# Adding up the modulation's partial sums: small TensorE products, or a round trip through device memory and VectorE

## The chip, the cores and the metric

The kernel runs on one core of one Trainium2 chip. The metric is device time in microseconds (us), the median of several runs. TensorE is called PE in the views of the profile, VectorE DVE, ScalarE ACT, GpSimd POOL, SyncE SP.

## The reference

A decoder trunk of two layers over a sequence of 256 rows of width 1024. Each layer has three sub-layers: a SwiGLU of width 2816, a token mixer (half spatial gating, half attention over selected keys), and a second SwiGLU. Each is normalised and modulated by a vector made from the condition `c`:

```
c_act = silu(c)
mod = c_act @ ada_w[l] + ada_b[l]                    # 1024 -> 9 * 1024
sh1, sc1, g1, sh2, sc2, g2, sh3, sc3, g3 = split(mod, 9)
h = rms_norm(x, norm) * (1 + sc) + sh
x = x + gate * sublayer(h)                           # gate is 0.5*g1, g2, 0.5*g3
```

The change concerns only `c_act @ ada_w`, a product of one row with a matrix of 1024 x 9216 per layer.

## The kernel before, in words

**The stream of weights.** All weights come in an order that is fixed in a list (`seq`). SP loads them in tiles of 128 x 1024 into seven buffers (`raw`). A tile of a matrix product is split in two parts: ScalarE rounds it to the coarser format (`whi`, line 535), and VectorE computes the rest (`wlo`, line 540). Both go into a ring of ten slots (`NB`), a slot being free again when the second half of the sequence has used it. PE multiplies with three products for each pair of tiles (high by high, high by low, low by high).

**The two halves.** The 256 rows are two halves of 128, 0 and 1. In the up projections of a SwiGLU (`joint_chunk`) both are multiplied together, 256 columns wide; in the down projection and the mixer they go apart, half 0 up to seven items ahead of half 1 (`LAG`), after which the halves alternate. One step of such a generator is an item: one weight tile for one half (in the joint part for both). In the down projection an item is six matmuls.

**The modulation.** Vector by vector (A is the scale, B the shift, G the gate, with the number of the sub-layer), eight tiles of `ada_w` stand between the weight tiles in the list. Partition p holds the rows 8p to 8p+7 of the matrix, so each engine operation multiplies a tile by a column of `c_act` and adds it to an accumulator `aacc` of 128 x 1024 (ScalarE's line 517 for the first, VectorE's line 522 for the others). What is left is to add `aacc` over the 128 partitions. Layer 0's A1 and B1 are made in `start` in another way; the other sixteen vectors, ten of kind A or B and six of kind G, are finished as follows.

- `fold_rows` (line 409): two items after the last tile, VectorE's transposing reduce (line 414) turns `aacc` into `R`, 128 x 32: within each block of 32 partitions the sums over those 32, so that four partial sums stand on four groups of partitions.
- Ten items later PE multiplies `R` by a constant 0/1 matrix `fold`, which adds the four groups: `col_finish` (line 458) for A and B, whose result has to stand with the width over the partitions, and `ada_finish` (line 423) for G. The result lies in a PSUM bank.
- One item after that VectorE takes it out. For A and B it picks each partition's own quarter (lines 466, 469) and adds bias and norm weight (`col_bias`). For G it adds a row of biases, loaded earlier by POOL (line 420), POOL writes the row to device memory (`gline`, line 435) and loads it back spread to all partitions (`vec`, line 437), and the residual update uses it (line 645).

Work like this is put off with `defer(n, ...)`: it is written into the program n items later. The program order is therefore fixed by these counts; each engine carries out its own instructions in that order.

**What stands around it.** In the first SwiGLU of layer 0 POOL also makes the tables of the rotary embedding, one step after each item (`rope_tables`, lines 179 to 227): POOL and VectorE take turns (the tile `nf` is written by POOL, line 194, and cast by VectorE, lines 196 and 198). There too the weights of the spatial gating are loaded and masked by POOL (`sgu_prep`, line 877) and transposed by PE some items later (line 885, four matmuls of line 117 on `xm`). POOL also computes the reciprocal roots of the norms (line 618). PSUM has eight banks, handed out in turn by `take` and `give`; the gates of the SwiGLU empty them (lines 797 and 798).

**Line 575 and PE's streams.** `mm3r` writes 512 columns in a strided order; after any other matmul, or after 48 of its own (`PERIOD`), it puts in one group in plain order, with the second product cut in two of 256 columns.

Of the kernel before, what the change touches and what calls it, by code (L numbers as in the profile page):

```python
# [9 lines left out]
F32 = mybir.dt.float32  # L10
# [3 lines left out]
ALU = mybir.AluOpType  # L14
AX = mybir.AxisListType

P = 128
D = 1024
KD = D // P
# [10 lines left out]
SPREAD = (1, 2, 1)  # L30
TAIL = 3
VX = 188
FOLD_D = (2, 2, 10)
ADA_DL = 8
D_EVP = 0
D_V = 0
# [4 lines left out]
EV_D = 1  # L41
# [60 lines left out]
def trunk(ctx, tc, x_in, c_in, pos_in, ada_w, ada_b, norm_ffn1, ffn1_w_in, ffn1_w_out,  # L102
# [3 lines left out]
    V, S, G = nc.vector, nc.scalar, nc.gpsimd  # L106
# [11 lines left out]
    T = Counted()  # L118
    ctx.enter_context(tc.manual_schedule())
    const = ctx.enter_context(tc.tile_pool(name="const", bufs=1))  # L120
    small = ctx.enter_context(tc.tile_pool(name="small", bufs=2))
# [3 lines left out]
    vecp = ctx.enter_context(tc.tile_pool(name="vecp", bufs=NV))  # L125
    dramp = ctx.enter_context(tc.tile_pool(name="dramp", bufs=2, space=bass.MemoryType.DRAM))
# [10 lines left out]
    def give(*ts):  # L137
        banks.extend(ts)
# [5 lines left out]
    ident = const.tile([P, P], F32, name="ident")  # L144
# [4 lines left out]
    S.activation(ccol, c_raw, AF.Silu)  # L149
    negm = const.tile([P, 2 * P], F32, name="negm")  # L150
    V.memset(negm, 1.0)
    fold = const.tile([P, P], F32, name="fold")
    mconst = const.tile([P, 16], F32, name="mhalf")
    mhalf, quarter = mconst[:, :1], mconst[:, 4:8]
    G.memset(mhalf, -0.5)

    def fold_setup():
        V.tensor_reduce(quarter, ident.rearrange("p (a c) -> p a c", a=4), axis=AX.X, op=ALU.add)
        V.tensor_reduce(fold[:, :32], ident.rearrange("p (a c) -> p c a", a=4), axis=AX.X, op=ALU.add)
        V.tensor_copy(fold[:, 32:].rearrange("p (a c) -> p a c", a=3),  # L160
                      fold[:, None, :32].to_broadcast([P, 3, 32]))

    def causal_mask():
        G.memset(negm, 0.0)
# [66 lines left out]
    cols = const.tile([P, DEPTH, 96], F32, name="cols")  # L231
    ab = const.tile([P, DEPTH, 3, 2, KD], F32, name="ab")
    accs = [None]
# [14 lines left out]
    def spare_tile(i):  # L248
        n_sp[i] += 1
        q = n_sp[i] % 3  # L250
        return spare[i][:, 32 * q:32 * q + 32]
# [100 lines left out]
    vec = {}  # L352
    pend = []

    def defer(n, fn):
        pend.append([n, fn])
# [49 lines left out]
                    :, j, v * D:(v + 1) * D])  # L406
            dp[0] += 1

    def fold_rows(acc, then):
        R = spare_tile(0)  # L410
        blocks = acc.rearrange("p (j r) -> p j r", r=32)

        def red():
            V.tensor_reduce(R, blocks, axis=AX.X, op=ALU.add, apply_transpose=True)
            then(R)
        defer(FOLD_D[0], red)

    def bias_row(e):
        row = spare_tile(1)[:32]
        G.dma_start(row, ada_b[e["l"], e["v"] * D:(e["v"] + 1) * D].rearrange("(j r) -> j r", r=32))  # L420
        accs.append(row)

    def ada_finish(e, acc):
        l, v = e["l"], e["v"]
        row = accs.pop()

        def go(R):
            def prod():
                ps = tp_tile()
                T.matmul(ps[:32, :32], R, fold[:, :32], start=True, stop=True)  # L430

                def put():
                    V.tensor_tensor(row, ps[:32, :32], row, op=ALU.add)
                    line = dramp.tile([1, D], F32, name="gline", tag="gline")
                    G.dma_start(line.rearrange("o (j r) -> (o j) r", r=32), row)
                    t = vecp.tile([P, D], F32, name="vec", tag="vec")
                    G.dma_start(t, line.to_broadcast([P, D]))
                    vec[(l, "G", v // 3 + 1)] = t
                evac_later(EV_D, put)
            defer(FOLD_D[2], prod)  # L440
        fold_rows(acc, go)

    have = set()

    def col_bias(l, i, kind, cs, k0):
        n = cs.shape[-1]
        v = (i - 1) * 3 + (kind == "A")
        bias = cols[:, l, v * KD + k0:v * KD + k0 + n]
        have.add((l, i, kind))
        if kind == "A":  # L450
            gn = cols[:, l, 72 + (i - 1) * KD + k0:72 + (i - 1) * KD + k0 + n]
            dst = ab[:, l, i - 1, 0, k0:k0 + n]
            V.scalar_tensor_tensor(dst, cs, 1.0, bias, op0=ALU.add, op1=ALU.add)
            V.tensor_tensor(dst, dst, gn, op=ALU.mult)
        else:
            V.tensor_tensor(ab[:, l, i - 1, 1, k0:k0 + n], cs, bias, op=ALU.add)

    def col_finish(e, acc, late):
        def go(R):
            def prod():  # L460
                ps = tp_tile()
                T.matmul(ps[:, :32], fold, R, start=True, stop=True)

                def put():
                    Rk = R.rearrange("p (k m) -> p k m", m=4)
                    V.tensor_tensor(Rk, ps[:, :32].rearrange("p (k m) -> p k m", m=4),
                                    quarter[:, None, :].to_broadcast([P, KD, 4]), op=ALU.mult)
                    cs = small.tile([P, KD], F32, name="cs", tag="cs")
                    V.tensor_reduce(cs, Rk, axis=AX.X, op=ALU.add)
                    col_bias(e["l"], e["v"] // 3 + 1, e["kind"], cs, 0)  # L470
                evac_later(EV_D, put)
            defer(FOLD_D[2] + late, prod)
        fold_rows(acc, go)

    late = []

# [11 lines left out]
    def pump(quota=2, force=False, now=False, hi_only=False):  # L488
        dma_fill()
        if hold[0] > 0 and not (force or now):  # L490
            return
        if not hi_only:
            pump_lo()
        while sp[0] < len(seq) and quota > 0:
            e = seq[sp[0]]
            if hi_only and e["k"] != "w":
                break
            if e["k"] == "s":
                if "done" not in e:
                    break  # L500
                sp[0] += 1
                continue
            need = e["k"] == "w"
            r = len(ring)
            if e["k"] == "w" and not force and len(W) - wcur[0] >= lead[0]:
                break
            if need and r >= NB and not ring[r - NB]:
                assert not force, (r, ring[r - NB:], wcur, [q[0] for q in pend])
                break
            if e["k"] == "a":  # L510
                j = e["j"]
                if j == 0:
                    aacc = accs[0] = aap.tile([P, D], F32, name="aacc", tag="aacc")
                    if e["kind"] == "G":
                        bias_row(e)
                    if ADA0_ACT:
                        S.activation(aacc, e["raw"], AF.Copy, scale=ccol[:, 0:1])
                    else:
                        V.tensor_scalar(aacc, e["raw"], ccol[:, 0:1], None, op0=ALU.mult)
                else:  # L520
                    aacc = accs[0]
                    V.scalar_tensor_tensor(aacc, e["raw"], ccol[:, j:j + 1], aacc,  # L522
                                           op0=ALU.mult, op1=ALU.add)
                if j == KD - 1 and e["kind"] == "G":
                    ada_finish(e, aacc)
                elif j == KD - 1:
                    col_finish(e, aacc, ADA_DL if (e["kind"], e["v"]) == ("A", 7) else 0)
            if need:
                ring.append(False)
                hi = hlp.tile([P, D], F32R, name="whi", tag="whi")  # L530
                lo = hlp.tile([P, D], F32R, name="wlo", tag="wlo")
                n = e["kt"] * e["cols"]
                src = e["raw"][:, :n]
                quota -= 1
                S.activation(hi[:, :n], src, AF.Copy)  # L535
                if hi_only:
                    late.append((e, hi, lo, r))
                    sp[0] += 1
                    continue
                V.tensor_tensor(lo[:, :n], src, hi[:, :n].bitcast(F32), op=ALU.subtract)  # L540
                e["hi"], e["lo"], e["slot"] = hi, lo, r
                W.append(e)
            sp[0] += 1
            n_rd[0] += 1
            dma_fill()
# [302 lines left out]
    def tp_tile():  # L848
        m = tp_n[0]
        tp_n[0] += 1  # L850
        if m - 2 in tp_ev:
            tp_ev.pop(m - 2)()
        t = tp_bank[m] = take()
        return t

    def evac_later(n, fn, tiles=1):
        done = []
        mine = range(tp_n[0] - tiles, tp_n[0])

        def run():  # L860
            if not done:
                done.append(1)
                fn()
                give(*[tp_bank.pop(m) for m in mine])
        for m in mine:
            tp_ev[m] = run
        if n is not None:
            defer(n, run)
        return run
# [393 lines left out]
    def start(env):  # L1263
# [73 lines left out]
        next(gb)  # L1337
        hold[0] = 0
        causal_mask()
        fold_setup()  # L1340

    gens = {}
    for pi, (kind, l, i, n) in enumerate(phases):
# [89 lines left out]
```

## Time and profile before

| | us |
|---|---|
| median of 3 runs | 979.49 |
| lowest, highest | 978.81, 979.78 |
| the profiled execution | 978.13 |
| its span in the trace | 976.40 |
| PE busy | 961.0 (98%) |
| VectorE busy | 768.7 (79%) |
| ScalarE busy | 530.1 (54%) |
| GpSimd busy | 54.8 (6%) |

The granted clock of TensorE was 0.999 of full speed. All moments are microseconds from the span's start. A row of the timeline gives start, duration, engine, line, operation, what it writes and reads, and, where the engine stood idle before, how long and what ended it. Matmuls overlap, so that two rows' starts, not their durations, tell how fast PE goes. A row of the stretches gives for each engine the busy time and the count of instructions, then the granted clock, the busy share of the DMA engines and the rate in GB/s. A row of the DMA issues gives the count, the size and the median time from issue to landing.

### The profile page before, as it was taken

Reading aid. Unit: us, or ns where it says so; the run is one execution under the profiler, and the core shown is the slowest. Engines: PE = TensorE matmul, PEld = TensorE weight load, DVE = VectorE, ACT = ScalarE, POOL = GpSimd, SP = SyncE. Lnnn points to the kernel's source line nnn. Section 1 sums busy time; section 2 is a strip of 40 time slices with the busy share of each in tenths; the row PEclk is TensorE's granted clock in tenths of the full one; section 3 lists DMA queues with packets and bytes.
Section 4 is the critical chain, followed back from the end, with each engine's and each line's share of the span. In section 5 each row is a group of like instructions: output and inputs, shape, how many; then the busy total and the mean of one; then the engine's idle time right before and its main releaser. Section 6 shows DMA issues by size and latency. Waiting matters only on the chain.

```text
span 976.4 us, 16690 instructions
## 1 busy us (share of the span) xinstructions
PE 961.0 (98%) x6448; PEld 866.6 (89%) x6448; DVE 768.7 (79%) x1072; ACT 530.1 (54%) x794; POOL 54.8 (6%) x92
## 2 busy tenths in 40 slices
PE   7999999999999999999999999999999999999997
PEld 6899998887888899998889999988777889999886
DVE  6889899788998888786587898767899886656444
ACT  6565555375676754553366554345657775444331
POOL 4012400000000100000000100000000000000000
PEclk9999999999999999999999999999999999999999
DMA  9989999967665799897868999885765557777431
GB/s 330 393 277 364 337 385 377 413 178 230 185 181 172 229 329 348 314 328 252 262 185 299 329 332 318 302 301 173 246 189 184 170 175 250 247 239 235 151 129 43
DMA packets 110416, 253.47 MB, mean 260 GB/s; under 512 B 9138, under 2 KB 27620, under 8 KB 110336
## 3 DMA queue, kind: packets, MB, share of 16 engines
q1 hardware_dynamic: 108256, 248.06, 74.6%
q0 software_dynamic: 1792, 3.82, 1.2%
q8 instruction: 50, 0.82, 0.3%
q10 hardware_dynamic: 288, 0.52, 0.1%
q14 instruction: 30, 0.25, 0.1%
HBM read 251.30 MB, written 1.07 MB: 258 GB/s over the span
## 4 chain that ended last, share of the span: by engine, by line
PE 85%; DVE 6%; DMA 4%; issue 2%; ACT 1%; POOL 0%; SPq 0%; POOLq 0%; DVEq 0%; ACTq 0%
PE bank L113 83%; PE bank L117 2%; DMA raw<-in_ffn_w_in_dram 2%; DVE wlo L540 2%; DMA sraw<-in_ada_w_dram 1%; DVE aacc L1195 1%; DVE aacc L522 1%; ACT whi L535 1%; DMA raw<-in_ada_w_dram 1%; DVE xm L645 0%; DVE xm L635 0%; DVE x L647 0%; DVE wlo L481 0%; POOL rstd L618 0%; DVE hTlo L641 0%
## 5 line engine op out<-in xcount | busy, mean ns | idle before, releaser
L535 ACT ACTIVATE whi<-raw 128x1024 fp32r<-128x1024 f32 (+1 forms) x328 | 340.2, 1050 | 261.9 <-PE bank L113 167.1
L540 DVE TENSOR_TENSOR wlo<-raw,whi 128x1024 fp32r<-128x1024 f32 (+1 forms) x313 | 375.1, 1211 | 112.1 <-ACT whi L535 110.6
L113 PE MATMUL bank<-hThi,whi 128*128 128x256 f32 x1216 | 325.0, 278 | 1.4 <-ACT hThi L1233 0.9
L113 PE MATMUL bank<-hThi,wlo 128*128 128x256 f32 x1216 | 322.0, 276 | 0.0
L113 PE MATMUL bank<-hTlo,whi 128*128 128x256 f32 x1216 | 322.0, 276 | 0.0
L113 PEld LDWEIGHTS bank<-hThi,whi 128*128 128x128 f32 x1216 | 222.4, 188 | 3.5 <-ACT hThi L1233 1.5
L113 PEld LDWEIGHTS bank<-hTlo,whi 128*128 128x128 f32 x1216 | 222.1, 188 | 0.1
L113 PEld LDWEIGHTS bank<-hThi,wlo 128*128 128x128 f32 x1216 | 222.0, 188 | 0.0
L522 DVE SCALAR_TENSOR_TENSOR aacc<-raw,ccol,aacc 128x1024 f32<-128x1024 f32 x112 | 143.5, 1281 | 0.0
L113 PE MATMUL bank<-whi,aThi 128*128 128x512 f32 (+1 forms) x374 | 141.0, 377 | 0.0
L113 PE MATMUL bank<-whi,hThi 128*128 128x512 f32 (+1 forms) x352 | 140.4, 399 | 0.0
L113 PE MATMUL bank<-wlo,aThi 128*128 128x512 f32 (+1 forms) x404 | 140.1, 359 | 0.0
L113 PE MATMUL bank<-whi,aTlo 128*128 128x512 f32 (+1 forms) x374 | 139.8, 374 | 0.0
L113 PE MATMUL bank<-whi,hTlo 128*128 128x512 f32 (+1 forms) x352 | 135.4, 385 | 0.2
L113 PE MATMUL bank<-wlo,hThi 128*128 128x512 f32 (+2 forms) x374 | 134.3, 369 | 0.0
L113 PEld LDWEIGHTS bank<-wlo,aThi 128*128 128x128 f32 x404 | 75.9, 188 | 13.0
L113 PEld LDWEIGHTS bank<-wlo,hThi 128*128 128x128 f32 x374 | 70.5, 188 | 12.1
L113 PEld LDWEIGHTS bank<-whi,aTlo 128*128 128x128 f32 x374 | 70.3, 188 | 11.1
L113 PEld LDWEIGHTS bank<-whi,aThi 128*128 128x128 f32 x374 | 70.2, 188 | 10.9
L113 PEld LDWEIGHTS bank<-whi,hTlo 128*128 128x128 f32 x352 | 66.1, 188 | 14.0 <-DVE hTlo L641 1.1
L113 PEld LDWEIGHTS bank<-whi,hThi 128*128 128x128 f32 x352 | 66.3, 188 | 13.6 <-issue 2.0
L798 DVE TENSOR_TENSOR xm<-xm,bank 128x256 f32<-128x256 f32 x76 | 29.6, 417 | 38.8 <-ACT xm L797 38.8
(166 smaller groups left out, 680.9 us busy)
## 6 DMA issues: line engine op xcount, KB each, us to landing
raw<-in_ffn_w_in_dram SPq DMA_DIRECT2D x160, 512.0 KB, 5.4
raw<-in_ada_w_dram SPq DMA_DIRECT2D x128, 512.0 KB, 5.5
raw<-in_ffn_w_out_dram SPq DMA_DIRECT2D x88, 512.0 KB, 5.8
raw<-in_mix_w_in_dram SPq DMA_DIRECT2D x40, 512.0 KB, 4.4
sraw<-in_ada_w_dram SPq DMA_DIRECT2D x32, 256.0 KB, 5.8
raw<-in_ffn_w_in_dram SPq DMA_DIRECT2D x32, 256.0 KB, 4.2
raw<-in_mix_w_out_dram SPq DMA_DIRECT2D x16, 512.0 KB, 4.1
vec<-gline POOLq DMA_DIRECT2D x6, 512.0 KB, 7.2
```

The source lines that it names most:

```text
L113: return nc.tensor.matmul(*a, **kw)
L117: return nc.tensor.transpose(*a, **kw)
L522: V.scalar_tensor_tensor(aacc, e["raw"], ccol[:, j:j + 1], aacc, op0=ALU.mult, op1=ALU.add)
L535: S.activation(hi[:, :n], src, AF.Copy)
L540: V.tensor_tensor(lo[:, :n], src, hi[:, :n].bitcast(F32), op=ALU.subtract)
L798: V.tensor_tensor(a, a, acc[j][:, 256:], op=ALU.mult)
L1195: V.scalar_tensor_tensor(acc, su[g][j], ccol[:, j:j + 1], su["dps"] if j == PEJ else acc, op0=ALU.mult, op1=ALU.add)
```

## The change

The products with `fold` go, and with them the constants `fold` and `quarter`, their setup, the bank that each took, and the loading of the bias rows. In their place `column_sums`, for all sixteen vectors: behind the transposing reduce POOL writes `R` to a table `part` in device memory, 128 x 32, and with four loads, one for each quarter of the columns, brings to every partition the four partial sums of its own eight columns (`C`, 128 x 32, pieces of 32 bytes). Eleven items after the reduce (`FOLD_D[1]`; nineteen for A3, which was put off by eight items before as well) VectorE adds the four. For A and B `col_bias` follows as before. For G the bias is added there from the columns `cols`, a transpose on VectorE brings the result to rows of 32, and POOL writes it to `gline` with four DMAs instead of one.

```
-FOLD_D = (2, 2, 10)
+FOLD_D = (2, 11)
...
-    def fold_rows(acc, then):
-        R = spare_tile(0)
-        blocks = acc.rearrange("p (j r) -> p j r", r=32)
+    def column_sums(acc, then, late=0):
+        R, C = spare_tile(0), spare_tile(1)
 
         def red():
-            V.tensor_reduce(R, blocks, axis=AX.X, op=ALU.add, apply_transpose=True)
-            then(R)
+            V.tensor_reduce(R.rearrange("p (m k) -> p m k", m=4),
+                            acc.rearrange("p (k m r) -> p m k r", m=4, r=32),
+                            axis=AX.X, op=ALU.add, apply_transpose=True)
+            part = dramp.tile([P, 32], F32, name="part", tag="part")
+            G.dma_start(part, R)
+            src = part.rearrange("(g r) (m k) -> m r g k", g=4, m=4)
+            for m in range(4):
+                G.dma_start(C[32 * m:32 * m + 32].rearrange("p (g k) -> p g k", g=4), src[m])
+
+            def total():
+                cs = small.tile([P, KD], F32, name="cs", tag="cs")
+                V.tensor_reduce(cs, C.rearrange("p (g k) -> p k g", g=4), axis=AX.X, op=ALU.add)
+                then(cs, C)
+            defer(FOLD_D[1] + late, total)
         defer(FOLD_D[0], red)
...
     def ada_finish(e, acc):
         l, v = e["l"], e["v"]
-        row = accs.pop()
...
-                ps = tp_tile()
-                T.matmul(ps[:32, :32], R, fold[:, :32], start=True, stop=True)
...
+        def put(cs, C):
+            Z = spare_tile(0)
+            V.tensor_tensor(C[:, :KD], cs, cols[:, l, v * KD:(v + 1) * KD], op=ALU.add)
+            V.transpose(Z, C)
+            line = dramp.tile([1, D], F32, name="gline", tag="gline")
+            dst = line.rearrange("o (k m r) -> m (o k) r", m=4, r=32)
+            for m in range(4):
+                G.dma_start(dst[m], Z[32 * m:32 * m + KD])
+            t = vecp.tile([P, D], F32, name="vec", tag="vec")
+            G.dma_start(t, line.to_broadcast([P, D]))
+            vec[(l, "G", v // 3 + 1)] = t
+        column_sums(acc, put)
...
     def col_finish(e, acc, late):
...
+        column_sums(acc, lambda cs, C: col_bias(e["l"], e["v"] // 3 + 1, e["kind"], cs, 0), late)
```

In the program order ScalarE's and SP's instructions are as before, and VectorE's large ones stand where they stood. PE has the sixteen small products fewer; its plain groups (`mm3r`) come at other places behind that, and its banks in another turn. On POOL the five DMAs of a sum stand behind the reduce that they wait for; those of the first sum (A2) stand in the midst of the rotary tables' steps. The rows are shown in the prediction at the two places of which it speaks, which lie in the first SwiGLU of layer 0.

More of the change, by code (lines that the diff above doesn't have):

```diff
@@ L151, in trunk @@
     V.memset(negm, 1.0)
-    fold = const.tile([P, P], F32, name="fold")
     mconst = const.tile([P, 16], F32, name="mhalf")
-    mhalf, quarter = mconst[:, :1], mconst[:, 4:8]
+    mhalf = mconst[:, :1]
     G.memset(mhalf, -0.5)
[L157 to L161, printed above, removed]
     def causal_mask():
@@ L416, in fold_rows @@
         defer(FOLD_D[0], red)
[L418 to L421, printed above, removed]
     def ada_finish(e, acc):
         l, v = e["l"], e["v"]
-        row = accs.pop()
-        def go(R):
-            def prod():
-                ps = tp_tile()
-                T.matmul(ps[:32, :32], R, fold[:, :32], start=True, stop=True)
[L432 to L441, printed above, removed]
+        def put(cs, C):
[9 more added lines that the diff above has]
+            vec[(l, "G", v // 3 + 1)] = t
@@ L458, in col_finish @@
     def col_finish(e, acc, late):
[L459 to L473, printed above, removed]
+        column_sums(acc, lambda cs, C: col_bias(e["l"], e["v"] // 3 + 1, e["kind"], cs, 0), late)
     late = []
@@ L513, in pump @@
                     aacc = accs[0] = aap.tile([P, D], F32, name="aacc", tag="aacc")
-                    if e["kind"] == "G":
-                        bias_row(e)
                     if ADA0_ACT:
@@ L1339, in start @@
         causal_mask()
-        fold_setup()
     gens = {}
```

## The prediction

> **What bounds the kernel now.** I read the page first (span, busy shares, the chain that ended last), then a table of stretches, then single rows in order of time around the places the change touches.
>
> ```profile
> span 976.4 us, 16690 instructions
> PE 961.0 (98%) x6448; PEld 866.6 (89%) x6448; DVE 768.7 (79%) x1072; ACT 530.1 (54%) x794; POOL 54.8 (6%) x92
> PE 85%; DVE 6%; DMA 4%; issue 2%; ACT 1%; POOL 0%; SPq 0%; POOLq 0%; DVEq 0%; ACTq 0%
> ...
> 110.00:150.00 40.00, 40.00 (x346) 39.66 (x346) 39.83 (x49) 23.23 (x31) 2.20 (x3) 1.00 0.97 360
> ```
>
> TensorE (PE) is the bound: 961.0 of 976.4 us busy, 85% of the chain. So a product taken off PE is worth its whole time. But in the first phase VectorE has nothing in hand: 39.83 of 40 us busy from 110 to 150, the DMA engines at 0.97 of theirs (last columns: clock, DMA share, GB/s). A wait of VectorE there is not made up.
>
> **What a product costs.** Rows of PE: a column product (A or B) among 256-wide matmuls, then a gate product (G) among 512-wide ones, and the last matmul of the stretch behind it.
>
> ```profile
> 103.20 0.28 PE L113 MATMUL bank<-hThi,wlo 128*128 128x256 f32 x1
> 103.31 0.30 PE L113 MATMUL bank<-hThipad,fold 128*128 128x32 f32 x2
> 103.45 0.36 PE L113 MATMUL bank<-hThi,whi 128*128 128x256 f32 x1
> 103.65 0.28 PE L113 MATMUL bank<-hTlo,whi 128*128 128x256 f32 x1
> ...
> 447.88 0.39 PE L113 MATMUL bank<-whi,aTlo 128*128 128x512 f32 x1
> 448.20 0.25 PE L113 MATMUL bank<-fold,hThipad 128*32 128x32 f32 x2
> 448.38 0.50 PE L113 MATMUL bank<-whi,aThi 128*128 128x512 f32 x1
> 448.71 0.40 PE L113 MATMUL bank<-wlo,aThi 128*128 128x256 f32 x2
> 448.94 0.40 PE L113 MATMUL bank<-whi,aTlo 128*128 128x512 f32 x1
> 459.09 0.39 PE L113 MATMUL bank<-whi,aThi 128*128 128x512 f32 x1
> ...
> 479.85 0.40 PE L113 MATMUL bank<-whi,aTlo 128*128 128x512 f32 x1
> 490.59 0.40 PE L113 MATMUL bank<-whi,aThi 128*128 128x512 f32 x1
> ```
>
> Starts count. Column: 103.20 to 103.65 is 0.45 us where two steps of 0.113 belong: 0.225 too much. Gate: 448.94 to 459.09 is 46 steps of 0.22; 447.88 to 448.94 is 1.06 for three of them: 0.40 too much. Ten column and six gate products: 10 x 0.225 + 6 x 0.40 = 4.65 us. (Four column products lie among 512-wide matmuls; I use the same price.) Behind one gate product the stream is slower: 479.85 to 490.59, 46 steps too, takes 10.74 against 10.15. I count 0.6 us as gained there; bounds 0 and 0.6.
>
> **VectorE's own work.** Removed per column sum: an add and a reduce; now one reduce of 128 x 32. Per gate: one add before; now a reduce, an add and a transpose of 128 x 32, which no row shows. Bounds: 0.17 (the small add at 171.07, below) and 1.24 (the transposing reduce at 84.78, below); I take 0.2, the size of the small ones.
>
> ```profile
> L469 DVE TENSOR_REDUCE cs<-hThipad 128x8 f32<-128x32 f32 x10 | 1.9, 186 | 0.3
> ```
>
> So 10 x -0.19 + 6 x 0.39 is near +0.4 us in sixteen places: nothing by itself. The one-off setup of fold at the end of start goes; I count nothing for it.
>
> **The new transfers on POOL.** Each sum now has five DMAs where it had none (gates, beside these, four writes for one; the bias loads go). The reads wait in POOL's queue until the write has landed, and whatever POOL has behind them waits too. First place, POOL before, in the first phase: nf is the rope tables' operand.
>
> ```order
> L880 AFFINE_SELECT xm_109<-xm_109 128x512
> L188 TENSOR_SCALAR ang<-invt,posf 128x8
> L194 TENSOR_SCALAR nf<-ang 128x16
> L201 TENSOR_SCALAR t_1042<-nf 128x16
> L202 TENSOR_TENSOR ang<-ang,t_1042 128x16
> ```
>
> POOL now (part is the table in device memory, hTlopad the receiving tile):
>
> ```order
> L859 AFFINE_SELECT xm_108<-xm_108 128x512
> L410 DMA part<-hThipad 128x32
> L413 DMA hTlopad<-part 32x4x8 x4
> L181 TENSOR_SCALAR ang<-invt,posf 128x8
> L187 TENSOR_SCALAR nf<-ang 128x16
> L194 TENSOR_SCALAR t_1044<-nf 128x16
> ```
>
> The five DMAs of the first sum (A2) have come in ahead of the table's steps. VectorE at the same place, now (L406 is the transposing reduce, L777 empties a bank; before, the same order stood there):
>
> ```order
> L406 TENSOR_REDUCE hThipad<-aacc 128x32
> L189 CAST ni<-nf 128x16
> L191 CAST nf<-ni 128x16
> L777 TENSOR_TENSOR xm_107<-xm_107,bank_80 128x256
> L777 TENSOR_TENSOR xm_107<-xm_107,bank_86 128x256
> L519 TENSOR_TENSOR wlo<-raw,whi 128x1024
> ```
>
> The first cast needs nf; behind it stands the emptying of bank_80, which PE's next transposes (the gating weights) write. The rows of before:
>
> ```profile
> 79.63 0.31 POOL L188 TENSOR_SCALAR ang<-invt,posf 128x8 f32<-128x8 f32 x1
> 80.03 0.26 POOL L194 TENSOR_SCALAR nf<-ang 128x16 f32<-128x16 f32 x1
> ...
> 84.78 1.24 DVE L414 TRANSPOSE_TENSOR_REDUCE hThipad<-aacc 128x32 f32<-128x1024 f32 x1
> 85.94 0.13 DVE L196 CAST ni<-nf 128x16 int32<-128x16 f32 x1
> 86.19 0.74 DVE L798 TENSOR_TENSOR xm<-xm,bank 128x256 f32<-128x256 f32 x2
> ...
> 89.26 0.60 PE L117 MATMUL bank<-ident,xm 128*128 128x128 f32 x4
> ```
>
> Before, nf was ready 5.6 us ahead of the cast. Now POOL begins the write only behind the reduce. Prices, from issue to landing in us (last number) and an issue of 128 pieces:
>
> ```profile
> hTlopad<-in_ada_b_dram POOLq DMA_DIRECT2D x2, 4.0 KB, 4.4
> ...
> gline<-hTlopad POOLq DMA_DIRECT2D x2, 4.0 KB, 6.3
> ...
> gline<-hTlopad POOLq DMA_DIRECT2D x1, 4.0 KB, 1.6
> ...
> 11.94 1.13 POOL L175 DMA_DIRECT2D posi<-in_positions_dram  x2
> ```
>
> The first is from 110 to 135 us, the second from 160 to 200, the third from 935 to 955, where the queues are empty. In the full stretch I take 5.4 for the write (between 4.4 and 6.3) and 4.4 for the reads (a read); 0.56 per issue.
>
> A2: reduce ends 86.02; write issued 0.29 later (the gap between gate add and gline issue, rows below), 86.31; landed 91.7; four issues from 91.8, 2.24, to 94.05; ang and nf 0.66 (79.63 to 80.29): 94.7. Cast at 94.75 instead of 85.94: VectorE is 8.8 late. Bank_80 is emptied 0.62 later, 95.4; PE's transposes start then instead of at 89.26: **PE waits 6.1 us**.
>
> **Second place: gate G2.** Its reduce and its sum lie close together. VectorE before (bank_82 holds G1's product, bank_87 G2's):
>
> ```order
> L414 TENSOR_REDUCE hThipad<-aacc 128x32
> L433 TENSOR_TENSOR hTlopad<-bank_82,hTlopad 32x32
> L540 TENSOR_TENSOR wlo<-raw,whi 128x1024 x2
> L522 SCALAR_TENSOR_TENSOR aacc<-raw,ccol,aacc 128x1024
> L540 TENSOR_TENSOR wlo<-raw,whi 128x1024 x2
> L522 SCALAR_TENSOR_TENSOR aacc<-raw,ccol,aacc 128x1024
> L433 TENSOR_TENSOR hTlopad<-bank_87,hTlopad 32x32
> L540 TENSOR_TENSOR wlo<-raw,whi 128x1024
> ```
>
> And now:
>
> ```order
> L406 TENSOR_REDUCE hThipad<-aacc 128x32
> L417 TENSOR_REDUCE cs<-hTlopad 128x8
> L427 TENSOR_TENSOR hTlopad<-cs,cols 128x8
> L428 STREAM_TRANSPOSE hThipad<-hTlopad 128x32
> L519 TENSOR_TENSOR wlo<-raw,whi 128x1024 x2
> L501 SCALAR_TENSOR_TENSOR aacc<-raw,ccol,aacc 128x1024
> L519 TENSOR_TENSOR wlo<-raw,whi 128x1024 x2
> L501 SCALAR_TENSOR_TENSOR aacc<-raw,ccol,aacc 128x1024
> L417 TENSOR_REDUCE cs<-hTlopad 128x8
> L427 TENSOR_TENSOR hTlopad<-cs,cols 128x8
> L428 STREAM_TRANSPOSE hThipad<-hTlopad 128x32
> L519 TENSOR_TENSOR wlo<-raw,whi 128x1024
> ```
>
> The second L417 has six large operations to hide two transfers behind; the wlo behind it is what PE needs.
>
> ```profile
> 147.91 0.40 PE L113 MATMUL bank<-whi,aThi 128*128 128x512 f32 x1
> ...
> 162.91 1.25 DVE L414 TRANSPOSE_TENSOR_REDUCE hThipad<-aacc 128x32 f32<-128x1024 f32 x1
> ...
> 164.51 0.50 POOL L435 DMA_DIRECT2D gline<-hTlopad  x1 [47.25 <-DVE hTlopad L433]
> 170.88 0.56 POOL L437 DMA_DIRECT2D vec<-gline  x1 [5.88 <-DMA gline<-hTlopad]
> 170.55 1.06 ACT L535 ACTIVATE whi<-raw 128x1024 fp32r<-128x1024 f32 x1 [2.06 <-PE bank L113]
> 171.07 0.17 DVE L433 TENSOR_TENSOR hTlopad<-bank,hTlopad 32x32 f32<-32x32 f32 x1
> 171.64 1.23 DVE L540 TENSOR_TENSOR wlo<-raw,whi 128x1024 fp32r<-128x1024 f32 x1 [0.40 <-ACT whi L535]
> ```
>
> When PE needs the wlo of 171.64: an item of the down projection is six steps, 1.33 us, from 147.91. Half 0 runs seven items ahead, then halves alternate. The whi of 170.55 waited for PE to leave a ring slot: 17 items after 147.91 half 1 has left tile 4, so with ten slots this is tile 14. Half 0 takes it as item 22, at 177.2, its wlo at 177.3. Done at 172.87: 4.4 us in hand.
>
> After the change, 8.8 late: reduce ends 164.16 + 8.8 = 172.96; write issued 173.25, landed 178.65; last of four read issues starts 0.1 + 3 x 0.56 later, 180.4; landed 184.8. VectorE is there at 179.9 and waits 4.9. Sum, add, transpose 0.55, wlo 1.23: 186.6 against 177.3, **9.3 us late in all**. That holds the first 6.1: PE is at VectorE's mercy here, and the two column and two gate products before it save nothing.
>
> **The sum.** 9.3, less the twelve later products (8 x 0.225 + 4 x 0.40 = 3.4), less 0.6: +5.3 us. The other fourteen sums are not reached: the shortest distance from reduce to sum is that of a gate at 467 us, 12.8, against 1.24 + 0.29 + 4.4 + 0.1 + 1.68 + 4.4 = 12.1, and no table step stands behind their transfers.
>
> ```profile
> 467.33 1.24 DVE L414 TRANSPOSE_TENSOR_REDUCE hThipad<-aacc 128x32 f32<-128x1024 f32 x1
> ...
> 480.11 0.17 DVE L433 TENSOR_TENSOR hTlopad<-bank,hTlopad 32x32 f32<-32x32 f32 x1
> ```
>
>  The profiled execution took 978.13 us (span 976.40 and 1.73 around it), 1.36 below the median of 979.49. 978.13 + 5.3 = 983.4 for its like; for the median **984.8**. Own range, by landings of 4.4 and of 6.3 throughout: +3.3 to +9.0, 982.8 to 988.5.
>
> The Trainium skill ("DMA: Bandwidth & Descriptors", Anatomy of one DMA — SWDGE (gpsimd) path) gives such a DMA about 2.0 us fixed. By that, an estimate from that page, PE would wait 2.7 us, G2's sum not at all, and the time would be 976.9. The loaded rows, 4.4 and 6.3, speak against it; the 1.6 at 941 us agrees.
>
> **Rivals.**
> - *Short landings, faster.* Landings of 1.6 as at 941 us: nf at 90.9, PE waits 2.3, VectorE 5.0 late; G2's sum at 174.5 finds its data before VectorE comes (176.1). 2.3 - 4.65 - 0.6 = -2.95: 976.5. For it: while VectorE stands, no weight buffers come free and traffic thins. Against it: the write lands in traffic already queued. It decides below about 2.5 us. Chance 0.13.
> - *Only the first wait reaches PE.* 6.1 - 4.65 - 0.6 = +0.85: 980.3. PE then needs the wlo at 177.3 + 6.1 - 1.25 = 182.2, so the two landings of G2 must sum to 5.4 where I have 9.8. Chance 0.15.
> - *The waits cost nothing*, some other bank serving the transposes: -5.25, 974.2. The order speaks against it. Chance 0.05.
> - *The clock falls too.* PE stands 6.1 and then about 4.5 us.
>
> ```profile
> 2.00:4.00 2.00, 2.00 (x11) 2.00 (x10) 0.00 (x0) 0.98 (x4) 1.77 (x4) 1.00 0.78 133
> 5.00:6.00 1.00, 1.00 (x11) 1.00 (x10) 0.00 (x0) 0.68 (x3) 0.00 (x0) 1.00 0.99 394
> 969.00:971.00 2.00, 0.38 (x4) 0.18 (x2) 1.93 (x7) 1.54 (x6) 0.00 (x0) 1.00 0.00 0
> 973.00:974.00 1.00, 0.00 (x0) 0.00 (x0) 0.00 (x0) 0.00 (x0) 0.00 (x0) 0.96 0.72 272
> ```
>
> The last matmul ends at 969.4, the granted clock falls near 973.9: 4.5 us of rest. At the start eleven transposes take 2 us, then 1 us: half pace for some 3.6 us costs 1.8. Behind A2 it is swallowed by G2; behind G2 it adds 1.8: 986.6, and 990.3 with the longest landings. The Trainium skill ("TensorE: Matmul & The Clock Gate", Part 1) lets one idle window of about 3.4 us do it; the one fall in the trace, 4.5 us after the last matmul, does not contradict that. Chance 0.10.
>
> **How the numbers follow.** Main 0.57, then 0.13, 0.15, 0.05, 0.10. A measurement tells 0.2% (2 us) from no change: same is 977.5 to 981.5, the one-wait case, 0.15; slower 0.57 + 0.10 = 0.67; faster 0.13 + 0.05 = 0.18. Range 976.4 to 990: it leaves out the free gain and the tails.
>
> **What would show it.** VectorE idle some 9 us before the cast behind the first transposing reduce, PE idle before the gating weights' transposes, VectorE idle about 5 us for a DMA at G2's sum, PE idle for a wlo behind it, sixteen products gone. If PE never waits near 89 and 180 us the forecast is wrong; if POOL reaches nf before 88, its first step is.

## The result and the profile after

The change made the kernel slower: 990.05 us (median of 4 runs, 989.61 to 992.08) against 979.57 of the kernel before on the same chip, a ratio of 1.0111 with a 95% interval of 1.0099 to 1.0123. The forecast was 984.8 with a range of 976.4 to 990.0. The direction was right, but the time lies just above the range, and the kernel lost twice as much as forecast (10.5 us against the forecast's 5.3). The profiled execution took 990.07 us, with a span of 988.4.

The page of the kernel after: the span, the busy shares and the chain that ended last.

```profile
span 988.4 us, 16768 instructions
PE 962.4 (97%) x6412; PEld 868.7 (88%) x6412; DVE 768.2 (78%) x1071; ACT 529.5 (54%) x794; POOL 108.3 (11%) x184
PE 83%; DVE 7%; DMA 4%; issue 3%; POOL 2%; ACT 1%; SPq 0%; POOLq 0%; DVEq 0%
```

PE has 36 instructions fewer than before (6448), VectorE as much to do, POOL twice as much. PE is still the bound by its share. The span is 12.0 us longer.

**The first place (A2).** POOL's rows of the kernel after, then VectorE's, then PE's:

```profile
84.33 0.57 POOL L410 DMA_DIRECT2D part<-hThipad  x1 [2.75 <-DVE hThipad L406]
90.19 2.22 POOL L413 DMA_DIRECT2D hTlopad<-part  x4 [5.29 <-DMA part<-hThipad]
92.44 0.32 POOL L181 TENSOR_SCALAR ang<-invt,posf 128x8 f32<-128x8 f32 x1
92.86 0.26 POOL L187 TENSOR_SCALAR nf<-ang 128x16 f32<-128x16 f32 x1
```

```profile
82.80 1.24 DVE L406 TRANSPOSE_TENSOR_REDUCE hThipad<-aacc 128x32 f32<-128x1024 f32 x1
93.15 0.18 DVE L189 CAST ni<-nf 128x16 int32<-128x16 f32 x1 [9.11 <-POOL nf L187]
...
93.44 0.75 DVE L777 TENSOR_TENSOR xm<-xm,bank 128x256 f32<-128x256 f32 x2
```

```profile
94.00 0.63 PE L117 MATMUL bank<-ident,xm 128*128 128x128 f32 x4 [3.01 <-POOL t L194]
```

The chain is as predicted: the write waits for the reduce, the reads for its landing, nf for the reads' issue, the cast for nf, the bank for the cast. VectorE stands 9.11 us. PE's transposes start at 94.00 instead of 89.26, 4.7 us later, but PE was idle for 3.01 us only: it had itself come late to them (see *PE's pace: kick*).

**The second place (G2).** The chain of waits of the kernel after, from 170 to 190 us (start, length, what), then the row of VectorE that waits and PE's row behind it:

```profile
171.60 5.57 DMA part<-hThipad
177.17 0.28 issue
177.46 1.33 POOL hTlopad L413 x3
178.79 0.30 issue
179.09 5.47 DMA hTlopad<-part
184.56 0.02 issue
184.59 0.22 DVE cs L417
...
185.16 1.20 DVE wlo L519
186.36 0.04 issue
186.40 3.77 PE bank L113 x15
```

```profile
184.59 0.21 DVE L417 TENSOR_REDUCE cs<-hTlopad 128x8 f32<-128x32 f32 x1 [5.83 <-DMA hTlopad<-part]
```

```profile
186.40 0.50 PE L113 MATMUL bank<-wlo,aThi 128*128 128x512 f32 x1 [2.06 <-DVE wlo L519]
```

Write, reads, sum, wlo, PE: the predicted chain again, and its end within 0.3 us (184.8 and 186.6 were forecast for the landing and the wlo). That it comes so close is luck: the write was issued 1.65 us earlier than forecast (171.60 for 173.25), and the two landings, 5.57 and 5.47, took 1.2 us more than the forecast's 5.4 and 4.4. They make up 11.0 of the 13.0 us from 171.60 to 184.56.

**The third place, which the prediction does not have: the end.** The last step on POOL in both kernels is the reciprocal root for the last rows (rstd); before it came at 971.29, and after:

```profile
976.76 0.60 POOL L597 TENSOR_TENSOR rstd<-ms,mhalf 128x1 f32<-128x1 f32 x1 [8.14 <-DVE ms L595]
```

That is 5.5 us later, and up to here the forecast of +5.3 holds. But the span grew by 12.0. So 6.5 us came in behind the last rstd, where little is left to compute. The stretches of the kernel after are empty from 980 us on (columns as in the prediction):

```profile
975.00:980.00 5.00, 0.00 (x0) 0.00 (x0) 2.73 (x9) 1.74 (x5) 0.60 (x1) 0.99 0.25 94
980.00:985.00 5.00, 0.00 (x0) 0.00 (x0) 0.00 (x0) 0.00 (x0) 0.00 (x0) 0.50 0.03 12
985.00:990.00 5.00, 0.00 (x0) 0.00 (x0) 0.00 (x0) 0.00 (x0) 0.00 (x0) 0.50 0.00 0
```

The instructions that end the program do not count as busy time, so neither the page nor the stretches show them. Among them is DRAIN, an instruction that each engine carries out at the end. They all have one source line (the end of the program text), and the view of that line gives for each kind: count, shortest, median and longest duration in ns, first and last start in us. Before:

```profile
L1429 POOLq DRAIN  x3: 46/93/3326, 971.3 to 976.1; - x3
L1429 SPq DRAIN  x3: 7/7/7, 975.6 to 975.9; - x3
```

and after:

```profile
L1407 POOLq DRAIN  x3: 46/102/10843, 976.7 to 988.1; - x3
L1407 SPq DRAIN  x3: 7/7/7, 981.0 to 987.8; - x3
```

SP's first DRAIN marks the moment when the last stores have landed: 975.6 and 981.0. POOL's first one is the long one, and starts with the last rstd. Before, it ended at 971.3 + 3.33 = 974.6, a microsecond ahead of the stores: hidden. After, it takes 10.84 us and ends at 987.6, 6.6 behind the stores, and all engines wait for it (SP's last DRAIN starts at 987.8; before, at 975.9).

### The profile page after: what moved, and what is told of

Same layout as the page of the kernel before. It is cut to its first block, busy times and chain, and to the rows that moved or that the text cites. A ratio compares the mean times of both kernels' runs of the same rounds, so it can differ in the third digit from the quotient of the medians.

```text
span 988.4 us, 16768 instructions
## 1 busy us (share of the span) xinstructions
PE 962.4 (97%) x6412; PEld 868.7 (88%) x6412; DVE 768.2 (78%) x1071; ACT 529.5 (54%) x794; POOL 108.3 (11%) x184
## 4 chain that ended last, share of the span: by engine, by line
PE 83%; DVE 7%; DMA 4%; issue 3%; POOL 2%; ACT 1%; SPq 0%; POOLq 0%; DVEq 0%
PE bank L113 81%; PE bank L117 2%; DVE wlo L519 2%; DMA sraw<-in_ada_w_dram 1%; DMA part<-hThipad 1%; DVE aacc L501 1%; DVE aacc L1174 1%; DMA raw<-in_ffn_w_in_dram 1%; POOL ang L181 1%; DMA hTlopad<-part 1%; DVE xm L624 0%; ACT whi L514 0%; DVE xm L614 0%; DVE x L626 0%; DVE wlo L462 0%
## 5 line engine op out<-in xcount | busy, mean ns | idle before, releaser
L113 PEld LDWEIGHTS bank<-whi,aThi 128*128 128x128 f32 x374 | 70.3, 188 | 11.5
L410 POOL DMA_DIRECT2D part<-hThipad x16 | 9.3, 579 | 496.7 <-DVE hThipad L406 482.6
```

The source lines that it names most:

```text
L113: return nc.tensor.matmul(*a, **kw)
L410: G.dma_start(part, R)
```

## The experiments

The table has the kernel after and ten experiments, each against runs of the kernel before on the same chip. The shifts are the moment of an rstd against that of the kernel before (202.19 at the end of the first SwiGLU, 971.29 for the last one), from one profiled execution each; "DRAIN" is POOL's at the very end.

| kernel | time | ratio to before, 95% | shift at 202 | shift at 971 | DRAIN | span |
|---|---|---|---|---|---|---|
| after | 990.05 | 1.0111 (1.0099 to 1.0123) | +7.85 | +5.47 | 10.84 | 988.4 |
| early_drain | 983.98 | 1.0051 (1.0036 to 1.0066) | +8.37 | +6.14 | 0.69 | 982.5 |
| kick | 989.99 | 1.0118 (1.0101 to 1.0135) | +7.86 | +5.50 | 10.84 | 988.4 |
| a2_only | 982.50 | 1.0038 (1.0025 to 1.0052) | +0.06 | -2.11 | 10.84 | 980.8 |
| g2_only | 987.84 | 1.0085 (1.0070 to 1.0101) | +5.57 | +3.47 | 10.84 | 986.4 |
| a2_g2 | 979.84 | 1.0015 (1.0002 to 1.0028) | -2.22 | -4.50 | 10.84 | 978.4 |
| all3 | 975.16 | 0.9959 (0.9947 to 0.9972) | -0.15 | -2.29 | 0.69 | 974.1 |
| all3_kick | 974.60 | 0.9959 (0.9946 to 0.9973) | -1.33 | -3.62 | 0.69 | 972.7 |
| b_dma92 | 984.45 | 1.0063 (1.0045 to 1.0082) | -0.06 | -0.19 | 10.84 | 982.7 |
| b_dma23big | 979.79 | 1.0011 (1.0002 to 1.0020) | +0.62 | +0.49 | 5.20 | 977.7 |
| b_dma92_drain | 979.51 | 1.0008 (0.9999 to 1.0017) | -0.31 | -0.37 | 1.60 | 976.0 |

Single executions of one kernel differ (977.37 to 980.23 us for the kernel before), and so do the profiled ones: early_drain, for one, has the same instructions as the kernel after up to 952 us, and its shift at 202 is 0.5 us larger. For all3 and a2_g2, the same up to 943 us, the shifts at 202 lie 2.1 us apart.

### The tail: early_drain

```
             vec[(l, "G", v // 3 + 1)] = t
+            if (l, v) == (1, 8):
+                G.drain()
```

> The changed kernel, with one DRAIN more on GpSimd behind its last load of a gate (951 us), where GpSimd is idle until 967. Tail theory: GpSimd's last DRAIN (10.84 us after the change, 3.33 before) works off something that each DMA issued by GpSimd leaves behind, and it ends 6.5 us behind the stores. Then the new DRAIN takes some 10 us beside other work, the last one under 3.3, and the time is 983.5 (990.05 - 6.5). Rival: the last DRAIN waits for something that happens at the end anyway; then it stays near 10.8 and the time at 990.

Measured 983.98, where the tail theory said 983.5 and its rival 990. The row of the new DRAIN, then the last one's:

```profile
L437 POOLq DRAIN  x1: 10793/10793/10793, 952.0 to 952.0; - x1
```

```profile
L1409 POOLq DRAIN  x3: 34/102/693, 977.4 to 982.3; - x3
```

The 10.8 us are the same, but lie at 952 to 963 beside PE's work, and the last DRAIN has 0.69 left, about what the rstd ahead of it takes (0.60). So it does not wait for the end of the program; it works off something that what ran before it has left. That this comes from the DMAs, the next three runs show.

### The tail: b_dma92, b_dma23big and b_dma92_drain

The kernel before, with DMAs that no one waits for:

```
+    dump = [dramp.tile([108, 32], F32, name="dump", tag="dump")]
+    def extra(q):
+        for n in range(3 if q < 20 else 2):
+            G.dma_start(dump[0][3 * q + n:3 * q + n + 1], ident[:1, :32])
...
+                    if pi == 2:
+                        extra(q)
```

> The kernel before, with 92 more DMAs on GpSimd (each one row of 128 bytes to device memory, issued two or three to an item in the up projection of the SwiGLU from 320 to 430 us; nothing waits for them). 92 is the number by which the change raises GpSimd's DMAs (32 to 124). Tail theory by the count of DMAs: the last DRAIN takes 10.8 us, the time is 979.6 + 6.5 = 986.1. Tail theory by the count of pieces moved (the change adds some ten thousand, this run 92): the DRAIN stays at 3.4, the time at 979.6. Rival, the tail has nothing to do with DMAs: 979.6 too, with the DRAIN at 3.3.

In b_dma23big the tile is 23 x 128 x 64 and the DMA another one:

```
+        if q < 23:
+            G.dma_start(dump[0][q].rearrange("p (a b) -> p a b", a=4)[:, :, :8],
+                        ident[:, :64].rearrange("p (a b) -> p a b", a=4)[:, :, :8])
```

> The kernel before, with 23 more DMAs on GpSimd in the same place, each of 512 pieces of 32 bytes (11,776 pieces, more than the change adds). By the count of DMAs (3.33 at 32, 10.84 at 124: 0.082 each) the last DRAIN takes 5.2 us, which ends some 0.8 us behind the stores: 980.0. By the count of pieces it takes 10.8 or more: 985.7.

The DRAIN of b_dma92, then of b_dma23big:

```profile
L1437 POOLq DRAIN  x3: 46/93/10839, 971.1 to 982.4; - x3
```

```profile
L1438 POOLq DRAIN  x3: 46/97/5201, 971.7 to 977.5; - x3
```

(The extra DMAs were issued from 320 to 402 us in b_dma92 and from 320 to 339 in b_dma23big, not up to 430.) 92 DMAs of a single row make the DRAIN as long as the change does (10.839 and 10.843), and the program up to the last rstd is as it was (-0.19). The 6.3 us by which its span grew are the tail alone. 23 DMAs of 512 pieces give 5.20, as the count of DMAs said (5.2), not the pieces (10.8 or more), and the time is 979.79, where the count said 980.0. Four kernels lie on one line: 32 DMAs 3.33, 55 DMAs 5.20, 124 DMAs 10.84 and 10.84; that is 0.082 us for each DMA and 0.7 besides. The median moved less than the span (984.45 where 986.1 was expected): the profiled execution of before, 978.13, lies 1.1 under the median of the runs beside these, and the profiled executions differ by 6.25 (984.38).

> The kernel before with the 92 small DMAs (984.45, its last DRAIN 10.84 us) and a DRAIN on GpSimd behind the last of them (430 us, GpSimd then idle to 490). If what the DMAs leave can be worked off at any time beside other work: the new DRAIN takes about 10.4 us (124 DMAs less the few that come later), the last one under 1.5, and the time is that of the kernel before, 979. If the last DRAIN counts all DMAs of the program again: 984.5.

This is b_dma92 with `G.drain()` behind the last extra DMA. The new DRAIN and the last:

```profile
L1349 POOLq DRAIN  x1: 11151/11151/11151, 401.3 to 401.3; - x1
```

```profile
L1439 POOLq DRAIN  x3: 46/98/1597, 970.9 to 975.8; - x3
```

979.51, the time of the kernel before. Twelve DMAs come behind the new DRAIN, and 0.7 + 12 x 0.082 = 1.7 is close to the 1.60 left. The 11.15 is 1.3 more than 112 DMAs would give by the same line. The last of them was issued at 401.35 us, as the DRAIN began; whether that is the reason is not shown.

### The two waits: a2_g2, a2_only and g2_only

```
-            for m in range(4):
-                G.dma_start(C[32 * m:32 * m + 32].rearrange("p (g k) -> p g k", g=4), src[m])
+            def reads():
+                for m in range(4):
+                    G.dma_start(C[32 * m:32 * m + 32].rearrange("p (g k) -> p g k", g=4), src[m])
+            if first:
+                defer(READ_D, reads)
+            else:
+                reads()
...
-        column_sums(acc, put)
+        column_sums(acc, put, 8 if (l, v) == (0, 5) else 0)
```

`first` is true for A2 of layer 0, `READ_D` is 4; (0, 5) is G2. The first part is a2_only, the second g2_only, both are a2_g2.

> The changed kernel, with A2's four loads written four items later (so that GpSimd makes nf ahead of them) and G2's sum eight items later. Theory of the two waits: PE's idle 3.0 us before 94.0 and 2.1 us before 186.4 go, VectorE no longer waits at either place, the time is 990.05 - 5.2 = 984.9. Rival: the first phase is held by the pace of PE's steps (118 ns against 113 before, from 51 to 155 us, some 4 us), which the waits only hide; then the waits go, but less than 1.5 us is gained: 988.5 or more. The tail stays in both.

> Of the two edits only A2's: its four loads written four items later. By the prediction's own steps G2's lateness of 9.3 us holds A2's 6.1, and without A2's wait G2's sum would still wait for its landing (reduce at 164.16, landed at 176.0, VectorE there at 171.1), but the wlo behind it is late by only 0.5: the gain is all but 0.5 of the 10.2 us of both, 980.3. Rival, the waits add up (3.0 us of idle PE before 94, 2.1 before 186): 990.05 - 3.0 to 5 = 985 to 987.

> Of the two edits only G2's: its sum eight items later. By the prediction's own steps A2's lateness of VectorE stays (7.4 us at ScalarE's and VectorE's instructions from 112 to 160 us in the trace after), PE is late by 6.1 from there, and G2's part is the 9.3 - 6.1 = 3.2 on top: 990.05 - 3.2 = 986.9, or 988 by the 2.1 us of idle PE that the trace shows before 186.4. Rival, G2 is the wait that counts: 982 or less.

Both edits together gain 10.2 us, twice what PE's idle time in the trace after adds up to (3.01 + 2.06 = 5.1, and 5.2 was my expectation). Both theories of a2_g2 were too low; the idle time of the bound engine is not what a wait costs. What the wait at A2 costs shows on VectorE. The same tile's wlo in the kernel before, in after and in kick (described below), some 20 us behind the cast:

```profile
109.34 1.23 DVE L540 TENSOR_TENSOR wlo<-raw,whi 128x1024 fp32r<-128x1024 f32 x1 [2.99 <-ACT whi L535]
```

```profile
116.65 1.23 DVE L519 TENSOR_TENSOR wlo<-raw,whi 128x1024 fp32r<-128x1024 f32 x1 [3.34 <-ACT whi L514]
```

```profile
116.81 1.23 DVE L519 TENSOR_TENSOR wlo<-raw,whi 128x1024 fp32r<-128x1024 f32 x1 [3.33 <-ACT whi L514]
```

It is 7.3 and 7.5 us late, and in early_drain 7.0, although PE stood idle at A2 for 3.01, 4.53 and 4.09 us in the three. While VectorE stands, no weight buffer comes free: SP waits 11.5 us for one wlo (from 80 to 100 us before, 2.4 at most), and the DMA share from 90 to 95 us is 0.08 (rows in the last part; before, 0.98). VectorE and the loads were both nearly full before, and the lateness is not made up: up to 155 us it stays between 6.8 and 7.9 us in all three. VectorE's cast in a2_g2, then PE's transposes:

```profile
85.70 0.17 DVE L190 CAST ni<-nf 128x16 int32<-128x16 f32 x1 [1.60 <-POOL nf L188]
```

```profile
89.38 0.60 PE L118 MATMUL bank<-ident,xm 128*128 128x128 f32 x4
```

VectorE's wait fell from 9.11 to 1.60, PE's transposes stand at 89.38 (before the change 89.26). One edit alone gives 7.5 us (a2_only) or 2.2 (g2_only), 9.7 together, so they nearly add up: A2's wait is three quarters of it. (These are differences of medians whose own 95% intervals reach 1.2 to 1.5 us to either side.) In a2_only PE still stands at G2:

```profile
178.37 0.49 PE L114 MATMUL bank<-wlo,aThi 128*128 128x512 f32 x1 [1.41 <-DVE wlo L526]
```

I had expected 980.3 there, with 0.5 us of lateness left at G2; it was 982.50, and G2's wait by itself costs 2.4 us (-2.11 against -4.50 at the last rstd). g2_only, 987.84, fell between the expected 986.9 and 988.

### PE's pace: kick

Between 51 and 89 us PE does nothing but equal steps in both kernels, but their number differs. The stretch before, then after:

```profile
51.00:89.00 38.00, 38.00 (x337) 38.00 (x336) 33.19 (x42) 22.73 (x33) 6.59 (x9) 1.00 0.92 320
```

```profile
51.00:89.00 38.00, 38.00 (x324) 37.98 (x324) 29.43 (x33) 22.82 (x33) 7.68 (x4) 1.00 0.93 327
```

38 us for 337 steps are 0.113 us each, for 324 they are 0.117, at a granted clock of 1.00 in both. Thirteen steps of 0.113 are 1.5 us, which is why PE was idle at A2 for less than its transposes were late.

```
-            T.transpose(ps[:, c * P:(c + 1) * P], su["acc"][:, o:o + P], ident)
+            for n in range(2 if (g, c) == (1, 3) else 1):
+                T.transpose(ps[:, c * P:(c + 1) * P], su["acc"][:, o:o + P], ident)
```

> The changed kernel, with one of the four transposes near 48 us made twice by PE (0.11 us), so that PE comes later to the matmul at 51.29 us that waited 0.09 us for hThi. Pace theory: it is that short wait that put PE's stream on 118 ns a step, on which it stayed to 155 us; without it the stream keeps 113.3 ns, about 900 steps of 4.5 ns are gained, 4.0 us, the time is 986.0. Rival: the pace follows from the change itself (the products are missing from the stream, or the tiles lie elsewhere): 118 ns again, 990.1.

Neither came out: the pace was the other one, the time did not change (989.99). The stretch in kick, the two around A2, and PE's row:

```profile
51.00:89.00 38.00, 38.00 (x337) 37.98 (x336) 29.66 (x33) 22.93 (x33) 7.68 (x4) 1.00 0.92 325
```

```profile
90.00:95.00 5.00, 0.82 (x5) 0.85 (x5) 1.64 (x5) 0.60 (x2) 3.82 (x9) 0.71 0.09 21
95.00:100.00 5.00, 5.00 (x30) 5.00 (x29) 5.00 (x7) 3.32 (x5) 3.27 (x5) 0.61 0.63 199
```

```profile
94.18 1.08 PE L117 MATMUL bank<-ident,xm 128*128 128x128 f32 x4 [4.53 <-POOL t L194]
```

PE comes early and waits longer, 4.53 us instead of 3.01; its transposes start at 94.18 (94.00 after). What sets that moment is VectorE's cast. The faster pace is worth nothing in front of a wait.

That the second transpose changed the pace is not shown. The same stretch in early_drain, which has the instructions of the kernel after up to 952 us and no second transpose:

```profile
51.00:89.00 38.00, 38.00 (x337) 37.99 (x336) 29.55 (x33) 22.92 (x33) 7.67 (x4) 1.00 0.93 328
```

It has the fast pace too. So the two paces occur with the same instructions, and also in the kernel before: b_dma23big, unlike it only from 320 us on, has 325 steps. Nor is the gain of a2_g2 its pace: kick and early_drain go as fast from 51 to 89 us and are 10.1 and 10.6 us later at 202.

### All together: all3 and all3_kick

Both waits avoided and the DRAIN at 943 us; all3_kick has the second transpose too.

> The two waits avoided (A2's loads four items later, G2's sum eight items later: 979.84 by themselves) and the DRAIN behind the last load of a gate as well. If the tail and the waits are separate costs, the DRAIN takes 6.5 us off: 979.84 - 6.5 = 973.3, 6 us (0.6%) under the kernel before. If the gain of the two waits came partly from the tail, or the DRAIN costs something elsewhere: 975 or more.

> The kernel with both waits avoided and the DRAIN (975.16), in which PE's steps took 118 ns from 51 to 89 us (1.5 us more than at 113.3), with one of the transposes near 48 us made twice (0.11 us), which set the other pace when it was tried in the changed kernel. If the pace counts where PE waits for nothing: steps of 113.3 ns from 51 us on, the time 975.16 - 1.6 to 1.8 = 973.4. If it sets the pace but the time stays at 975.2, PE is not the bound in this stretch. If the pace stays at 118 ns, this run tells nothing.

all3 beats both kernels: 975.16, 0.4% under the kernel before (0.28 to 0.53%). It is 1.9 us over the expected 973.3, but not by the DRAIN, which left 0.69: at the last rstd it was already 2.2 us later than a2_g2 (-2.29 and -4.50), and at 202 us by 2.1. The stretch from 51 to 89 us of all3, then of all3_kick:

```profile
51.00:89.00 38.00, 38.00 (x324) 37.98 (x324) 32.98 (x39) 24.60 (x36) 10.56 (x10) 1.00 0.93 325
```

```profile
51.00:89.00 38.00, 38.00 (x324) 37.99 (x324) 32.62 (x39) 24.36 (x35) 10.62 (x10) 1.00 0.93 327
```

all3 had the slow pace, a2_g2 the fast one (x337), though up to 943 us the two are the same program; that would be 1.5 us of the 2.1 that all3 was late at 202. That this is what the pace costs where PE waits for nothing is only argued: all3_kick was to show it, and its pace was slow as well (324 steps), so that it tells nothing of the pace. It came out level with all3 (974.60, the same ratio), yet its rstd at 202 came 1.2 us earlier, at the same pace. So why all3 misses 973.3 stays open.

## Where the prediction was right, and the step that failed

- *"PE waits 6.1 us" at A2.* The mechanism was right in each step: write landed after 5.9 from issue to the first read (5.4 was taken), four issues 2.22 (2.24), then ang and nf. The reduce came 2 us earlier than before (82.80), so nf was there at 93.1, not 94.7; the transposes were 4.7 late, not 6.1. The sum has G2's 9.3 hold the 6.1, so that G2 adds 3.2 to it, and by the same steps G2 without A2's wait costs 0.5. Measured, G2 costs 2.2 on top of A2 and 2.4 without it: each wait alone is worth what it is worth in the pair, within half a microsecond.
- *"9.3 us late in all" at G2.* At the end of that SwiGLU it was 7.85. The landings were 5.6 and 5.5 where I took 5.4 and 4.4, VectorE waited 5.83 for 4.9, and the wlo was done at 186.4 for 186.6. PE wanted the tile later than I had worked out: its matmul at 186.40 is 7.6 us later than its like before (178.8, not 177.3), so that its lateness there is 7.6 and not 9.3.
- *"less the twelve later products, 3.4, less 0.6".* From 7.85 at 202 us to 5.47 at 971: 2.4, not 4.0. The other kernels with the change gain 2.1 to 2.4 there as well. The price of a product was too high, or part of it came back as slower stretches; the runs do not part these. With the waits away, the sixteen products and the pace together gave 4.50 (a2_g2), 3.62 (all3_kick) and 2.29 (all3), for 5.25.
- *"+5.3 us".* +5.47 at the last rstd. That the sum is so close is luck: two errors of 1.5 us with opposite signs.
- *"978.13 + 5.3 = 983.4 for its like": this is the step that failed.* It carries the end of the program over as it was, without a reason given, and prices a DMA on POOL by its issue and its landing alone. Each of 92 more DMAs also left 0.082 us to POOL's last DRAIN, 7.5 us in all, of which 1.0 fitted ahead of the stores' landing as before: +6.5. With that term the sum for the profiled execution is 978.13 + 5.3 + 6.5 = 989.9; it took 990.07. Without the tail (early_drain) the kernel takes 983.98, where 984.8 was forecast. The row that could have told it was in the trace of before: a DRAIN of 3.33 us on an engine with 32 DMAs, a microsecond short of the end of the stores.
- *The other fourteen sums* cost nothing that shows: VectorE waits for a landing once in sixteen sums, as this group's row of the kernel after says (5.8 us of idle time in all).

```profile
L417 DVE TENSOR_REDUCE cs<-hTlopad 128x8 f32<-128x32 f32 x16 | 3.2, 200 | 5.8 <-DMA hTlopad<-part 5.8
L428 DVE STREAM_TRANSPOSE hThipad<-hTlopad 128x32 f32<-128x32 f32 x6 | 1.3, 211 | 0.2
```

  The transpose, estimated at 0.2 us, takes 0.21.
- *The rivals.* Short landings: the DMA issues of the kernel after from 930 to 955 us (count, KB each, us to landing) show 1.6 again for the gates' lines, but 3.0 for the write and 5.1 for the four loads even there.

```profile
hTlopad<-part POOLq DMA_DIRECT2D x4, 4.0 KB, 5.1
gline<-hThipad POOLq DMA_DIRECT2D x4, 1.0 KB, 1.6
part<-hThipad POOLq DMA_DIRECT2D x1, 16.0 KB, 3.0
```

  In the first phase the write took 5.6 at both places. The loads of A2, issued while VectorE stood and the weight loads had stopped, landed in 1.9: what the prediction said for this rival is true of the loads, and what it said against it is true of the write. At A2 only the write's landing counts. The Trainium skill's 2.0 us ("DMA: Bandwidth & Descriptors", Anatomy of one DMA — SWDGE (gpsimd) path) is near these 1.9 and the gates' 1.6; the 5.6 of the write disagree with it, and the measurement decides. Only the first wait reaching PE: no, G2's wait costs 2.2 to 2.4 alone. No cost at all: no. The clock: PE stood 3.01 and 2.06 us, and the granted clock stayed at 1.00, as these two stretches of the kernel after say:

```profile
90.00:95.00 5.00, 1.99 (x18) 1.82 (x17) 1.82 (x5) 0.78 (x2) 4.01 (x9) 1.00 0.08 13
...
185.00:190.00 5.00, 3.60 (x15) 2.93 (x16) 4.97 (x6) 0.25 (x1) 2.55 (x5) 1.00 0.39 120
```

  In kick, behind 4.53 us of rest, it fell to 0.71 and 0.61, and in early_drain, behind 4.09, to 0.88 and 0.78 in the same two stretches. In kick that cost nothing in the end, since G2's wait stood behind it: it is as late at 202 us as after. The rests with a fall and those without agree with the window of about 3.4 us that the Trainium skill gives ("TensorE: Matmul & The Clock Gate", Part 1).

## What to carry to other kernels

A DMA on GpSimd had a third price here, beside issue and landing: about 0.08 us at the end of the program for each one, the same for one row of 128 bytes and for 512 pieces of 32. It counts as soon as POOL's last DRAIN ends behind the last stores; the instructions that end the program show both moments. A DRAIN on GpSimd in a stretch where it is idle took that price off the end in each kernel that had one. What a wait costs is not the idle time of the bound engine beside it: here the lateness was that of VectorE and of the loads that wait for it, in a stretch where neither could make it up. In three executions that were almost equally late (7.85, 7.86 and 8.37 us at 202), PE stood idle at A2 for 3.01, 4.53 and 4.09 us; only undoing the waits showed the 10 us.

## What the runs showed of the hardware that was not expected

- POOL's DRAIN takes 0.7 us and 0.082 us for each DMA that POOL issued since the last DRAIN: 0.69 at none, 1.60 at 12, 3.33 at 32, 5.20 at 55, 10.84 at 124; 92 single rows count as much as the change's 92 DMAs. What it does in that time no run here shows. The Trainium skill ("VectorE: DVE Perf Modes", The DRAIN you can't avoid) calls the DRAINs at a program's start and end constant, some 12 ns on all five engines; if it means these, that fits SP's (7 ns) and not GpSimd's.
- PE's equal steps of 256 columns go at 0.113 or at 0.117 us, at a granted clock of 1.00, and keep the one or the other for tens of microseconds (after: 324 steps in 38 us; before and kick: 337). The same instructions went at the one in one execution and at the other in another (after and early_drain, all3 and a2_g2), so it is not the program alone that sets it. What does stays open.
